# Stick-breaking scores without the mask's matmul, a later multiply by the retention's row factors, and weights kept in the row tiles

## The chip, the cores and the metric

The kernel runs on one core of one Trainium2 chip. The metric is the device time of one execution in microseconds (us). TensorE (PE in the profile) multiplies matrices, VectorE (DVE) and ScalarE (ACT) do the elementwise work, GpSimd (POOL) a few small operations, and SyncE (SP) and ScalarE issue the transfers.

## The reference

Two layers. Each normalises the residual, multiplies it by one wide weight matrix, feeds the columns to four groups of heads (retention, Mamba-2 SSD, stick-breaking attention, a read of memory tokens), multiplies each group by its gate, and projects back. The change touches two of the groups:

```python
def stick_breaking(q, k, v):                 # 4 heads of 128, 512 positions, blocks of 128 queries
        logits = jnp.einsum('bthd,bshd->bhts', q_blk, k).astype(jnp.float32) * scale
        q_pos = i * SB_BLOCK + jnp.arange(SB_BLOCK)
        causal = key_pos[None, :] < q_pos[:, None]
        log_beta = jax.nn.log_sigmoid(logits)
        log_1mb = jnp.where(causal, jax.nn.log_sigmoid(-logits), 0.0)
        tail = lax.cumsum(log_1mb, axis=3, reverse=True) - log_1mb
        w = jnp.where(causal, jnp.exp(log_beta + tail), 0.0)
        return jnp.einsum('bhts,bshd->bthd', w.astype(v.dtype), v)

def retention(q, k, v):                      # 4 heads of 128; after y = intra + inter, per position and head:
    mu = jnp.mean(y, axis=-1, keepdims=True)
    var = jnp.mean(jnp.square(y - mu), axis=-1, keepdims=True)
    y = (y - mu) * lax.rsqrt(var + NORM_EPS)
```

A weight of stick-breaking is exp(logit minus the sum of softplus(logit) over the keys from this one up to the query, the query itself left out), and zero for keys at or behind the query.

## The kernel before

**Products.** Every product of float32 data is three matmuls: each operand is split into a rounded part h and a remainder l (`split`: ScalarE's cast, L286, then VectorE's subtraction, L287), and `mm3` adds h·h, h·l and l·h. Weights arrive as `raw` tiles of 1 MB, are split into `wh` and `wl` (128x1024 each), and a projection is a run of matmuls into a `pj` bank of PSUM; the heads' own products go to `mx` banks. There are four banks of each kind.

**Order.** The code is written in units of one projection. A head's later steps are put off by `defer(n, ...)`, which calls them n units later, so that projections stand between a head's steps. The tile framework then orders each engine's instructions by a list scheduler which plays the program through with its own cost table; the order on an engine is fixed before the program runs. An instruction waits for its data and, where it writes, for its tile's slot: `s` tiles have 33 slots, `y` 16 and `r` (the row tiles) 9.

**Stick-breaking head** (`sb_head`). The head's q is scaled and split (ACT L555, DVE L556), its k is split (L286, L287). For each block t of 128 queries, n = 128(t+1) keys: three matmuls give the logits in an `mx` bank, and a fourth, in bf16, multiplies an identity by a 128x128 block of large negative numbers above the diagonal and adds it on the diagonal block (L641). Then Abs (ACT L643), Exp and Ln (ACT L255), max(b,0)+u (DVE L646, softplus), the running sum from the last key back (DVE L647, a scan), b−u (DVE L649), and Exp (ACT L255). The four blocks' weights lie in three `s` tiles. Three units later they are transposed on PE (L661) and split, and a unit later multiplied by v.

**Retention head** (`ret_head2`, `ret_head3`). The head's y is copied (ACT L740), its squares are summed over the head's 128 channels: two halves added (DVE L744), split into z (ACT L746, DVE L747), and a matmul with a column of ones gives a row (`mx<-r,onesr`). `row_rstd` copies the row (ACT L707), sends it through SP as 32x16 (L709), adds eps and takes the power −1/2 on POOL (L710, L711), writes it to DRAM (L713) and reads it back to all 128 partitions as rB (L715, `r<-row`). Five units after the matmul `scaled` (L757) multiplies y by rB on VectorE. The heads' chains overlap, so L757 of one head stands in VectorE's queue beside L744 and L747 of a later one.

Other names in the rows: L696 to L699 rope; L808, L810, L813 the SSD convolution; L821 and L953 gates; L856, L857, L859 the SSD decay blocks (DVE, POOL, ACT); L730 the retention's causal select on POOL.

Of the kernel before, what the change touches and what calls it, by code (L numbers as in the profile page):

```python
# [8 lines left out]
F32 = mybir.dt.float32  # L9
# [3 lines left out]
ALU = mybir.AluOpType  # L13
# [3 lines left out]
P = 128  # L17
SEQ = 512
NT = SEQ // P
# [4 lines left out]
HEADS = 4  # L24
# [4 lines left out]
NEG = -1e30  # L29
# [94 lines left out]
    return np.ascontiguousarray(t.T.reshape(KC, P, -1).transpose(1, 0, 2).reshape(P, -1))  # L124


CO = dict(ident=0, tri=128, ones=256, neg=384, cos=512, sin=1024, ginv=1536, reps=1552)
NCON = 1552 + 64
RP, RJ = 32, 16


def shape_constants():
    c = np.zeros((P, NCON), np.float32)
    i = np.arange(P)
    c[:, 0:128] = np.eye(P)
    c[:, 128:256] = i[:, None] <= i[None, :]
    c[:, 256:384] = 1.0
    c[:, 384:512] = np.where(i[None, :] >= i[:, None], NEG, 0.0)
    inv = np.float32(10000.0) ** (-np.arange(0, HD, 2, dtype=np.float32) / np.float32(HD))
    ang = (np.arange(SEQ, dtype=np.float32)[:, None] * inv[None, :].astype(np.float32)).T  # L140
    c[:, 512:1024] = np.concatenate([np.cos(ang), np.cos(ang)])
    c[:, 1024:1536] = np.concatenate([np.sin(ang), -np.sin(ang)])
    gam = 1.0 - 2.0 ** (-5.0 - np.arange(HEADS, dtype=np.float64))
    m = np.arange(SEQ, dtype=np.float64)
    gi = gam[None, :] ** (-m[:, None]) * SCALE
    c[:, 1536:1552] = gi.reshape(NT, P, HEADS).transpose(1, 0, 2).reshape(P, 16)
    er = EPS * gam[None, :] ** (-2.0 * m[:, None])
    c[:RP, 1552:1616] = er.reshape(RP, RJ, HEADS).transpose(0, 2, 1).reshape(RP, HEADS * RJ)
    return c


# [4 lines left out]
class Pair:  # L156


    def __init__(self, K, cols=512, tag="s"):
        h, l = K.new(cols, F32R, tag), K.new(cols, F32R, tag)  # L160
        self.h, self.l, self.hf = h[:], l[:], h[:].bitcast(F32)
# [6 lines left out]
class Builder:  # L168
# [4 lines left out]
    def __init__(self, tc, pools, args, taps=None):  # L173
        self.tc, self.nc = tc, tc.nc
        self.a = args
        self.taps = taps or {}
        self.fix, self.slots, self.small, self.wp, self.ps, self.dr = pools
        self.n = self.unit = 0
        self.todo, self.tanhs = [], []
        self.C = self.fixed(NCON + DEPTH * NPAR, F32, "consts")  # L180
        self.b16 = self.fixed(2 * P, BF16, "b16")
        self.onesr = self.fixed(P, F32R, "onesr")
        self.mhalf = self.fixed(RJ, F32, "mhalf")
        self.eps4 = self.fixed(RJ, F32, "eps4")
        self.nc.gpsimd.memset(self.mhalf[:], -0.5)
        self.nc.gpsimd.memset(self.eps4[:], EPS)

# [46 lines left out]
    def con(self, name, n, parts=P):  # L234
        return self.C[:parts, CO[name]:CO[name] + n]

    def par(self, l, name, i, n=1):
        o = NCON + l * NPAR + PO[name] + i
        return self.C[:, o:o + n]
# [37 lines left out]
    def mm(self, out, lhsT, rhs, start, stop):  # L277
        return self.nc.tensor.matmul(out, lhsT, rhs, start=start, stop=stop)  # L278
# [350 lines left out]
    def sb_head(self, h, v):  # L629
        nc = self.nc  # L630
        q = self.scaled_pair(self.proj_b(), SCALE)
        k = self.pair(self.proj_b())
        w = [t[:, c] for t, c in self.packed([P * (t + 1) for t in range(NT)], self.buf)]
        for t in range(NT):
            n = P * (t + 1)
            ts = slice(P * t, P * t + P)
            b = self.mx()[:, :n]
            self.mm(b, q.h[:, ts], k.h[:, :n], True, False)
            self.mm(b, q.h[:, ts], k.l[:, :n], False, False)
            self.mm(b, q.l[:, ts], k.h[:, :n], False, False)  # L640
            self.mm(b[:, P * t:n], self.b16[:, 0:P], self.b16[:, P:2 * P], False, True)  # L641
            u = w[t]
            nc.scalar.activation(u, b, AF.Abs)  # L643
            self.act1(u, u, AF.Exp, scale=-1.0)
            self.act1(u, u, AF.Ln, bias=1.0)
            nc.vector.scalar_tensor_tensor(out=u, in0=b, scalar=0.0, in1=u, op0=ALU.max, op1=ALU.add)  # L646
            nc.vector.tensor_tensor_scan(out=u[:, ::-1], data0=u[:, ::-1], data1=u[:, ::-1], initial=0.0,  # L647
                                         op0=ALU.add, op1=ALU.bypass)
            nc.vector.tensor_sub(u, b, u)  # L649
            self.act1(u, u, AF.Exp)  # L650
        y = self.buf(tag="y")
        self.defer(3, self.sb_head2, h, v, w, y)
        return y
# [96 lines left out]
    def ret_head3(self, h, z, y):  # L750
        nc = self.nc
        vb = self.mx()[0:1]
        self.mm(vb, self.onesr[:, 0:1], z[:], True, True)
        self.defer(5, self.scaled, y, self.row_rstd(vb, self.con("reps", HEADS * RJ, RP)[:, RJ * h:RJ * h + RJ]))

    def scaled(self, y, rB):
        self.nc.vector.tensor_mul(y, y, rB)  # L757


    def dt_chain(self, l, u):  # L760
# [17 lines left out]
    def dt_sums(self, l, da, delta):  # L778
# [17 lines left out]
        hp = self.small.tile([P, 40], F32, tag="hp", name=self.name("hp"), bufs=2)[:]  # L796
        o = NCON + l * NPAR
        nc.vector.tensor_scalar(out=hp, in0=self.C[:, o:o + 40], scalar1=0.5, scalar2=None, op0=ALU.mult)
# [273 lines left out]
    def start(self):  # L1072

        nc = self.nc
        self.warm_up()
        nc.sync.dma_start(self.C[:, NCON:NCON + DEPTH * NPAR], self.a["params"])
        self.w_load(1)
        xs = [self.load_x(0)]
        self.w_load(2)
        preB = self.bcast_row(self.a["pre_norm_g"][0:1])  # L1080
        nc.sync.dma_start(self.C[:, 0:4 * P], self.a["consts"][:, 0:4 * P])
        xs += [self.load_x(1), self.load_x(2)]
        self.mem_tiles()
        self.w_prefetch(1)
        for i in range(4):
            self.mem_pairs(0, i)
        k = [self.pj(), self.pj()]

        def keys(h):
            self.proj_b(self.mx_, N_MEM, k[h // 2][:, N_MEM * (h % 2):N_MEM * (h % 2) + N_MEM])  # L1090
        keys(0)
        self.w_prefetch(2)
        self.w_load(3)
        xs.append(self.load_x(3))
        nc.sync.dma_start(self.C[:, 4 * P:NCON], self.a["consts"][:, 4 * P:NCON])
        keys(1)
        self.w_prefetch(4)
        self.w_load(4)
        keys(2)
        a = [self.normed_a(xs[0])]  # L1100
        self.w_prefetch(5)
        hn = [self.normed_b(a[0], preB)]
        keys(3)
        self.mem_squares()
        self.w_prefetch(6)
        self.mem_add()
        a.append(self.normed_a(xs[1]))
        hn.append(self.normed_b(a[1], preB))

        def v0():  # L1110
            a.append(self.normed_a(xs[2]))
            self.turned(hn[0], 0)
        v = [self.proj_a(self.mx_, 2, between=[v0])[0]]
        self.w_prefetch(7)
        hn.append(self.normed_b(a[2], preB))
        self.turned(hn[1], 1)
        a.append(self.normed_a(xs[3]))
        self.mem_cols()
        self.w_prefetch(8)
        hn.append(self.normed_b(a[3], preB))  # L1120

        def v1():
            self.turned(hn[2], 2)
        v.append(self.proj_a(self.mx_, 2, between=[v1])[0])
        row = self.to_rows(self.mcol, 2)
        self.w_prefetch(10)
        self.turned(hn[3], 3)
        nc.scalar.copy(self.mrow[:], row)
        self.w_load(5)
        for i in range(2):  # L1130
            self.mem_v2(v[i])
        self.w_prefetch(12)
        for i in range(2):
            self.mem_k2(k[i])
        self.w_load(6)
        nc.vector.tensor_copy(self.b16[:, 0:P], self.con("ident", P))
        nc.vector.tensor_copy(self.b16[:, P:2 * P], self.con("neg", P))
        nc.vector.tensor_copy(self.onesr[:], self.con("ones", P))

    def layer(self, l):  # L1140
# [32 lines left out]
def lay_out(x, mem, pre_norm_g, post_norm_g, w_in, conv_w, conv_b, dt_bias, a_log, d_skip, ssd_norm_g, mem_norm_g,  # L1173
            w_mem_kv, w_out):
    return {
        "x": x.reshape(SEQ, D),
        "memT": features_first(mem.reshape(N_MEM, D)),
        "pre_norm_g": pre_norm_g,
        "post_norm_g": post_norm_g,
        "wts": pack_weights(w_in, w_mem_kv, w_out),  # L1180
        "params": pack_params(conv_w, conv_b, dt_bias, a_log, d_skip, ssd_norm_g, mem_norm_g).reshape(P, DEPTH * NPAR),
        "consts": shape_constants(),
    }
# [14 lines left out]
```

## Time and profile before

| | |
|---|---|
| time, 3 runs | 961.94 us median (961.93 to 963.8) |
| profiled execution | 961.89 us, of which the span from the first to the last instruction is 960.2 us and 1.69 us lie outside |
| PE matmul, busy | 949.8 us (99% of the span), 5151 instructions |
| PE weight load | 812.6 us (85%) |
| DVE / ACT / POOL | 657.4 us (68%) / 456.8 us (48%) / 104.4 us (11%, 160 instructions) |
| granted TensorE clock | 0.998, 9 in every slice |

The busy time of PE counts matmuls that overlap, so it hides short gaps: a matmul's record is longer than the distance to the next one's start. Gaps are read from the starts in the timeline. In a row of the timeline the first number is the start, the second the duration, xN a run of N equal instructions, and brackets at the end give the time the engine stood idle before it and what released it.

### The profile page before, as it was taken

How to read it: one execution, taken by the hardware profiler on the slowest of the kernel's cores; microseconds unless marked ns; L12 is line 12 of the kernel's file. 1: busy time of each engine (PE TensorE's matmuls, PEld its weight loads, DVE VectorE, ACT ScalarE, POOL GpSimd, SP SyncE). 2: the span in 40 equal slices, each digit the busy share in tenths (PEclk: the TensorE clock that was granted, in tenths of full speed). 3: DMA queues.
4: the chain of work that ended last, by engine and by line, in shares of the span. 5: the costliest groups of instructions: out<-in, count | busy, mean ns of one | idle time of the engine just before them, and what ended most of it. 6: DMA issues, size and time to landing. Idle time of an engine off the chain costs nothing.

```text
span 960.2 us, 13253 instructions
## 1 busy us (share of the span) xinstructions
PE 949.8 (99%) x5151; PEld 812.6 (85%) x5151; DVE 657.4 (68%) x1056; ACT 456.8 (48%) x844; POOL 104.4 (11%) x160
## 2 busy tenths in 40 slices
PE   9999999999999999999999999999999999999997
PEld 7998889988887888888899888898888878888885
DVE  5855567767777796854487465768777968877443
ACT  6544566534554342643465345665344543435341
POOL 1100000001231201100040000000003421102001
PEclk9999999999999999999999999999999999999999
DMA  9442212122232524344344222112222333423502
GB/s 347 149 147 80 88 45 88 45 88 88 91 108 99 165 88 121 115 160 142 120 170 184 89 88 71 62 45 88 77 78 85 134 105 116 120 91 120 195 25 87
DMA packets 26734, 105.79 MB, mean 110 GB/s; under 512 B 4144, under 2 KB 4400, under 8 KB 17456
## 3 DMA queue, kind: packets, MB, share of 16 engines
q10 hardware_dynamic: 10224, 73.44, 21.8%
q1 hardware_dynamic: 16448, 31.52, 10.0%
q8 instruction: 40, 0.66, 0.3%
q14 instruction: 22, 0.18, 0.1%
HBM read 100.63 MB, written 4.28 MB: 109 GB/s over the span
## 4 chain that ended last, share of the span: by engine, by line
PE 88%; DVE 5%; DMA 3%; ACT 1%; issue 1%; POOL 1%; DVEq 0%; SPq 0%; ACTq 0%; POOLq 0%
PE pj L278 65%; PE mx L278 22%; DVE s L647 1%; DMA r<-row 1%; PE mx L599 1%; PE mx L449 1%; DMA mem<-memT 1%; DMA s<-acs 1%; DVE wl L287 1%; DMA t<-r 1%; POOL t L711 1%; DVE s L810 1%; DVE s L646 0%; PE mx L661 0%; DVE s L287 0%
## 5 line engine op out<-in xcount | busy, mean ns | idle before, releaser
L278 PE MATMUL pj<-hTh,wh 128*128 128x512 f32 x704 | 277.5, 394 | 0.0
L278 PE MATMUL pj<-hTl,wh 128*128 128x512 f32 x704 | 276.6, 393 | 0.0
L278 PE MATMUL pj<-hTh,wl 128*128 128x512 f32 x704 | 275.4, 391 | 0.0
L287 DVE TENSOR_TENSOR wl<-raw,wh 128x1024 fp32r<-128x1024 f32 (+2 forms) x155 | 183.7, 1190 | 114.2 <-ACT wh L286 107.3
L286 ACT CAST wh<-raw 128x1024 fp32r<-128x1024 f32 (+2 forms) x155 | 158.0, 1025 | 178.9 <-PE pj L278 153.7
L278 PEld LDWEIGHTS pj<-hTh,wl 128*128 128x128 f32 x704 | 132.3, 188 | 26.7
L278 PEld LDWEIGHTS pj<-hTh,wh 128*128 128x128 f32 x704 | 132.3, 188 | 26.4
L278 PEld LDWEIGHTS pj<-hTl,wh 128*128 128x128 f32 x704 | 132.4, 188 | 25.7
L278 PE MATMUL pj<-wh,s 128*128 128x512 f32 (+1 forms) x384 | 99.8, 355 | 0.0
L278 PE MATMUL mx<-s,s 128*128 128x256 f32 (+4 forms) x616 | 97.5, 310 | 0.3
L278 PEld LDWEIGHTS mx<-s,s 128*128 128x128 f32 (+1 forms) x616 | 84.6, 178 | 12.9 <-issue 3.1
L278 PE MATMUL mx<-wh,s 128*128 128x512 f32 x256 | 79.2, 389 | 0.0
L278 PEld LDWEIGHTS pj<-wh,s 128*128 128x128 f32 x384 | 66.1, 189 | 10.5
L730 POOL TENSOR_SCALAR_AFFINE_SELECT s<-s 128x128 fp32r<-128x128 f32 x64 | 21.2, 363 | 420.6 <-DVE s L287 420.6
L278 PE MATMUL pj<-wl,s 128*128 128x512 f32 (+1 forms) x192 | 63.4, 354 | 0.0
L278 PE MATMUL pj<-wh,hTh 128*128 128x256 f32 (+1 forms) x208 | 60.3, 290 | 0.5 <-DVE s L556 0.5
L287 DVE TENSOR_TENSOR s<-mx,s 128x512 fp32r<-128x512 f32 (+2 forms) x86 | 42.1, 517 | 26.0 <-ACT s L286 25.6
L278 PE MATMUL pj<-wl,hTh 128*128 128x256 f32 (+1 forms) x208 | 59.5, 286 | 0.0
L278 PE MATMUL pj<-wh,hTl 128*128 128x256 f32 (+1 forms) x208 | 58.5, 284 | 0.0
L278 PEld LDWEIGHTS mx<-wh,s 128*128 128x128 f32 x256 | 48.1, 188 | 10.0
L286 ACT CAST s<-mx 128x512 fp32r<-128x512 f32 (+2 forms) x86 | 36.7, 456 | 40.1 <-PE mx L278 24.1
L287 DVE TENSOR_TENSOR s<-y,s 128x512 fp32r<-128x512 f32 x64 | 41.3, 688 | 19.7 <-ACT s L286 14.0
(167 smaller groups left out, 1324.5 us busy)
## 6 DMA issues: line engine op xcount, KB each, us to landing
raw<-wts ACTq DMA_DIRECT2D x69, 1024.0 KB, 4.8
s<-x SPq DMA_DIRECT2D x24, 256.0 KB, 3.7
s<-acs SPq DMA_DIRECT2D x16, 256.0 KB, 6.1
raw<-wts SPq DMA_DIRECT2D x3, 1024.0 KB, 8.3
r<-row SPq DMA_DIRECT2D x12, 256.0 KB, 3.9
s<-acs SPq DMA_DIRECT2D x16, 128.0 KB, 6.7
x<-s SPq DMA_DIRECT2D x8, 256.0 KB, 2.0
out<-s SPq DMA_DIRECT2D x8, 256.0 KB, 2.0
```

The source lines that it names most:

```text
L278: return self.nc.tensor.matmul(out, lhsT, rhs, start=start, stop=stop)
L286: self.nc.scalar.copy(h, src)
L287: self.nc.vector.tensor_sub(l, src, hf)
L449: x = self.nc.tensor.transpose(b[:, P * j:P * j + P], hn[i][:, P * j:P * j + P], self.con("ident", P))
L599: nc.tensor.transpose(b[:, P * t:P * t + P], w[t // 2][:, o:o + P], self.con("ident", P))
L647: nc.vector.tensor_tensor_scan(out=u[:, ::-1], data0=u[:, ::-1], data1=u[:, ::-1], initial=0.0, op0=ALU.add, op1=ALU.bypass)
L711: nc.gpsimd.tensor_tensor(out=c, in0=c, in1=self.mhalf[:RP], op=ALU.pow)
L730: nc.gpsimd.affine_select(out=d, in_=d, pattern=[[1, P]], compare_op=ALU.is_ge, fill=0.0, base=0, channel_multiplier=-1)
L810: nc.vector.scalar_tensor_tensor(out=acc[:, s:], in0=b[:, :SEQ - s], scalar=tap(3 - s), in1=acc[:, s:], op0=ALU.mult, op1=ALU.add)
```

## The change

1. The mask's matmul (L641) is gone. The scan now multiplies the running sum by a row of ones and zeros (`run`, 512 new columns among the constants, in place of the 128 of `neg`) before it adds the next softplus, so that the sum starts anew at every key from the one just before the query on. After the last Exp, GpSimd's affine_select puts zeros at and above the diagonal of the diagonal block: 32 new POOL instructions of 128x128, and 32 matmuls with their 32 weight loads fewer. Two casts that filled `b16` at the start go too.
2. The weights lie in `r` tiles (9 slots) rather than `s` tiles (33), three a head.
3. `scaled` is put off by 7 units instead of 5, and is kept in program order.

The scheduler's order follows from these. Three places show it, all on VectorE in the first layer (the second repeats them). Names with numbers are tiles; the lines after the change are those of the new file, two or three higher from L661 on.

First place: the start of stick-breaking head 0. `wl270` is the l part of a weight tile, `s243` and `s249` are head 1's q and k, L646, L647, L649 head 0's chain. Before:

```order
L287 TENSOR_TENSOR wl270_1556<-raw214_1249,wh269_1555 128x1024
L646 SCALAR_TENSOR_TENSOR s229_1314<-mx232_1317,s229_1314 128x128
L647 SCALAR_TENSOR_TENSOR s229_1314<-s229_1314 128x128
L649 TENSOR_TENSOR s229_1314<-mx232_1317,s229_1314 128x128
L556 SCALAR_TENSOR_TENSOR s243_1406<-pj238_1374,s242_1405 128x512
L646 SCALAR_TENSOR_TENSOR s229_1314<-mx233_1329,s229_1314 128x256
L647 SCALAR_TENSOR_TENSOR s229_1314<-s229_1314 128x256
L646 SCALAR_TENSOR_TENSOR s230_1315<-mx234_1341,s230_1315 128x384
L649 TENSOR_TENSOR s229_1314<-mx233_1329,s229_1314 128x256
L287 TENSOR_TENSOR s249_1447<-pj245_1417,s248_1446 128x512
```

After:

```order
L556 SCALAR_TENSOR_TENSOR s243_1404<-pj238_1372,s242_1403 128x512
L287 TENSOR_TENSOR s249_1445<-pj245_1415,s248_1444 128x512
L287 TENSOR_TENSOR wl270_1554<-raw214_1247,wh269_1553 128x1024
L646 SCALAR_TENSOR_TENSOR r229_1312<-mx232_1315,r229_1312 128x128
L647 SCALAR_TENSOR_TENSOR r229_1312<-consts_72,r229_1312 128x128
L649 TENSOR_TENSOR r229_1312<-mx232_1315,r229_1312 128x128
L646 SCALAR_TENSOR_TENSOR r229_1312<-mx233_1327,r229_1312 128x256
L647 SCALAR_TENSOR_TENSOR r229_1312<-consts_72,r229_1312 128x256
L646 SCALAR_TENSOR_TENSOR r230_1313<-mx234_1339,r230_1313 128x384
```

Head 1's q and k (L556 and the L287 of s249) move ahead of head 0's whole chain, out of its middle.

Second place: the third retention head's sum of squares. `r507`, `r508` and `r509` are that head's, `y395` and `y426` the y of the first and the second head, `r439` and `r479` their rB, `wl540` a weight's l part. Before:

```order
L744 TENSOR_TENSOR r507_2836<-r507_2836,r508_2837 64x512
L757 TENSOR_TENSOR y426_2446<-y426_2446,r479_2700 128x512
L813 SCALAR_TENSOR_TENSOR s528_2949<-s528_2949,s527_2948 128x512
L810 SCALAR_TENSOR_TENSOR s532_2985<-pj529_2956,hp134_776,s532_2985 128x511
L810 SCALAR_TENSOR_TENSOR s532_2985<-pj529_2956,hp134_776,s532_2985 128x510
L747 TENSOR_TENSOR r509_2841<-r507_2836,r509_2841 64x512
L810 SCALAR_TENSOR_TENSOR s532_2985<-pj529_2956,hp134_776,s532_2985 128x509
L287 TENSOR_TENSOR wl540_3042<-raw490_2770,wh539_3041 128x1024
```

After (L746, L749, L760, L813 and L816 are what L744, L747, L757, L810 and L813 were):

```order
L816 SCALAR_TENSOR_TENSOR s528_2946<-s528_2946,s527_2945 128x512
L760 TENSOR_TENSOR y395_2290<-y395_2290,r439_2510 128x512
L813 SCALAR_TENSOR_TENSOR s532_2983<-pj529_2954,hp134_774,s532_2983 128x511
L746 TENSOR_TENSOR r507_2833<-r507_2833,r508_2834 64x512
L813 SCALAR_TENSOR_TENSOR s532_2983<-pj529_2954,hp134_774,s532_2983 128x510
L813 SCALAR_TENSOR_TENSOR s532_2983<-pj529_2954,hp134_774,s532_2983 128x509
L287 TENSOR_TENSOR wl540_3039<-raw490_2768,wh539_3038 128x1024
L749 TENSOR_TENSOR r509_2838<-r507_2833,r509_2838 64x512
L816 SCALAR_TENSOR_TENSOR s533_2984<-s533_2984,s532_2983 128x512
```

The multiply that stands here is now that of the first head (y395) and not of the second; `wl540` and one more instruction of the convolution, which stood behind L747, now stand ahead of L749.

Third place: the fourth retention head's sum of squares (`r535` to `r537`), before, where `y465` with `r522` is the third head's:

```order
L287 TENSOR_TENSOR wl561_3147<-raw526_2946,wh560_3146 128x1024
L757 TENSOR_TENSOR y465_2632<-y465_2632,r522_2915 128x512
L744 TENSOR_TENSOR r535_3008<-r535_3008,r536_3009 64x512
L813 SCALAR_TENSOR_TENSOR s558_3114<-s558_3114,s557_3113 128x512
L810 SCALAR_TENSOR_TENSOR s563_3152<-pj559_3121,hp134_776,s563_3152 128x511
L747 TENSOR_TENSOR r537_3013<-r535_3008,r537_3013 64x512
L810 SCALAR_TENSOR_TENSOR s563_3152<-pj559_3121,hp134_776,s563_3152 128x510
L810 SCALAR_TENSOR_TENSOR s563_3152<-pj559_3121,hp134_776,s563_3152 128x509
```

After:

```order
L287 TENSOR_TENSOR wl561_3145<-raw526_2943,wh560_3144 128x1024
L746 TENSOR_TENSOR r535_3005<-r535_3005,r536_3006 64x512
L816 SCALAR_TENSOR_TENSOR s558_3111<-s558_3111,s557_3110 128x512
L760 TENSOR_TENSOR y426_2444<-y426_2444,r479_2698 128x512
L813 SCALAR_TENSOR_TENSOR s563_3150<-pj559_3119,hp134_774,s563_3150 128x511
L749 TENSOR_TENSOR r537_3010<-r535_3005,r537_3010 64x512
L813 SCALAR_TENSOR_TENSOR s563_3150<-pj559_3119,hp134_774,s563_3150 128x510
```

L746 is no longer behind a multiply; the one that stands ahead of L749 is the second head's (y426 with r479), and the third head's comes nine rows behind L749.

On PE the matmul of the row (`mx<-r,onesr`) comes 8 projection matmuls earlier for the second head, 5 later for the third and 2 later for the fourth. On SP one of the loads of the SSD decay rows (`s<-acs`) moves ahead of the fourth head's `r<-row`.

The diff, cut to its core:

```diff
-CO = dict(ident=0, tri=128, ones=256, neg=384, cos=512, sin=1024, ginv=1536, reps=1552)
-NCON = 1552 + 64
+CO = dict(ident=0, tri=128, ones=256, run=384, cos=896, sin=1408, ginv=1920, reps=1936)
+NCON = 1936 + 64
...
-    c[:, 384:512] = np.where(i[None, :] >= i[:, None], NEG, 0.0)
+    c[:, 384:896] = np.arange(512)[None, :] < 383 + i[:, None]
...
-        w = [t[:, c] for t, c in self.packed([P * (t + 1) for t in range(NT)], self.buf)]
+        w = [t[:, c] for t, c in self.packed([P * (t + 1) for t in range(NT)], lambda: self.buf(tag="r"))]
+        run = self.con("run", SEQ)
...
-            self.mm(b, q.l[:, ts], k.h[:, :n], False, False)
-            self.mm(b[:, P * t:n], self.b16[:, 0:P], self.b16[:, P:2 * P], False, True)
+            self.mm(b, q.l[:, ts], k.h[:, :n], False, True)
...
-            nc.vector.tensor_tensor_scan(out=u[:, ::-1], data0=u[:, ::-1], data1=u[:, ::-1], initial=0.0,
-                                         op0=ALU.add, op1=ALU.bypass)
+            nc.vector.tensor_tensor_scan(out=u[:, ::-1], data0=run[:, SEQ - n:][:, ::-1], data1=u[:, ::-1], initial=0.0,
+                                         op0=ALU.mult, op1=ALU.add)
             nc.vector.tensor_sub(u, b, u)
             self.act1(u, u, AF.Exp)
+            d = u[:, P * t:]
+            nc.gpsimd.affine_select(out=d, in_=d, pattern=[[-1, P]], compare_op=ALU.is_gt, fill=0.0, base=0, channel_multiplier=1)
...
-        self.defer(5, self.scaled, y, self.row_rstd(vb, self.con("reps", HEADS * RJ, RP)[:, RJ * h:RJ * h + RJ]))
+        self.defer(7, self.scaled, y, self.row_rstd(vb, self.con("reps", HEADS * RJ, RP)[:, RJ * h:RJ * h + RJ]))
 
     def scaled(self, y, rB):
-        self.nc.vector.tensor_mul(y, y, rB)
+
+        self.tc.keep_in_program_order(self.nc.vector.tensor_mul(y, y, rB))
...
-        nc.vector.tensor_copy(self.b16[:, 0:P], self.con("ident", P))
-        nc.vector.tensor_copy(self.b16[:, P:2 * P], self.con("neg", P))
```

## Rows read from the trace of the kernel before

**Rows 1.** The page: busy time of each engine, share of the span, instructions.

```profile
PE 949.8 (99%) x5151; PEld 812.6 (85%) x5151; DVE 657.4 (68%) x1056; ACT 456.8 (48%) x844; POOL 104.4 (11%) x160
```

**Rows 2.** Waits of PE: line waited for, total us, times, longest us.

```profile
PE mx L278 <- DVE r L747: 1.8, 2, 0.9
```

**Rows 3.** Timeline of PE around a mask of stick-breaking head 0.

```profile
136.82 0.39 PE L278 MATMUL pj<-hTh,wh 128*128 128x512 f32 x1
137.05 0.44 PE L278 MATMUL mx<-s,s 128*128 128x128 f32 x3
137.34 0.23 PE L278 MATMUL mx<-b 128*128 128x128 bf16 x1
137.38 0.47 PE L278 MATMUL pj<-hTl,wh 128*128 128x512 f32 x1
137.69 0.51 PE L278 MATMUL mx<-s,s 128*128 128x256 f32 x3
```

**Rows 4.** Timeline of PE at two stops of the stick-breaking stage.

```profile
149.81 0.51 PE L278 MATMUL mx<-s,s 128*128 128x256 f32 x3
150.57 0.38 PE L278 MATMUL pj<-wh,hTh 128*128 128x256 f32 x1 [0.24 <-DVE s L556]
150.79 0.28 PE L278 MATMUL pj<-wl,hTh 128*128 128x256 f32 x1
150.91 0.28 PE L278 MATMUL pj<-wh,hTl 128*128 128x256 f32 x1
...
165.84 0.27 PE L661 MATMUL mx<-consts,s 128*128 128x128 f32 x1
166.23 0.73 PE L278 MATMUL mx<-s,s 128*128 128x512 f32 x2
```

**Rows 5.** Timeline of DVE ahead of the first of these stops.

```profile
149.82 0.69 DVE L556 SCALAR_TENSOR_TENSOR s<-pj,s 128x512 fp32r<-128x512 f32 x1 [0.85 <-ACT s L555]
```

**Rows 6.** Timeline of PE at the fourth retention head's row.

```profile
307.41 0.39 PE L278 MATMUL pj<-hTl,wh 128*128 128x512 f32 x1
308.69 0.39 PE L278 MATMUL mx<-r,onesr 128*1 128x512 f32 x1 [0.89 <-DVE r L747]
```

**Rows 7.** Timeline of DVE ahead of the third and the fourth head's row.

```profile
285.19 1.12 DVE L757 TENSOR_TENSOR y<-y,r 128x512 f32<-128x512 f32 x1
...
288.39 0.69 DVE L747 TENSOR_TENSOR r<-r,r 64x512 fp32r<-64x512 f32 x1
...
305.37 0.69 DVE L757 TENSOR_TENSOR y<-y,r 128x512 f32<-128x512 f32 x1 [5.42 <-DMA r<-row]
...
307.95 0.69 DVE L747 TENSOR_TENSOR r<-r,r 64x512 fp32r<-64x512 f32 x1
```

**Rows 8.** Timeline of ACT: the fourth head's squares, which L744 adds.

```profile
298.60 1.19 ACT L743 ACTIVATE r<-mx 64x512 f32<-64x512 f32 x2
```

**Rows 9.** Timeline of PE at the third head's row.

```profile
290.53 0.40 PE L278 MATMUL mx<-r,onesr 128*1 128x512 f32 x1
```

**Rows 10.** Line L730: duration ns min/median/max, first and last start.

```profile
L730 POOL TENSOR_SCALAR_AFFINE_SELECT s<-s x64: 284/294/1262, 216.9 to 750.6; 128x128 fp32r<-128x128 f32 x64
```

**Rows 11.** Groups by line and form: busy us, mean ns | idle before.

```profile
L287 DVE TENSOR_TENSOR wl<-raw,wh 128x1024 fp32r<-128x1024 f32 x145 | 177.1, 1224 | 110.9 <-ACT wh L286 104.2 <-PE mx L278 6.2
L647 DVE TENSOR_TENSOR_SCAN s<-s 128x512 f32<-128x512 f32 x8 | 9.8, 1219 | 0.0
```

**Rows 12.** Timeline of POOL and DVE where selects meet a weight's split.

```profile
257.72 2.32 POOL L730 TENSOR_SCALAR_AFFINE_SELECT s<-s 128x128 fp32r<-128x128 f32 x3
257.78 1.31 DVE L287 TENSOR_TENSOR wl<-raw,wh 128x1024 fp32r<-128x1024 f32 x1
```

**Rows 13.** Windows: us, busy PE, PEld, DVE, ACT, POOL (instructions), clock, DMA, GB/s.

```profile
160.00:180.00 20.00, 19.89 (x160) 19.00 (x160) 16.24 (x29) 14.14 (x31) 0.00 (x0) 1.00 0.17 56
```

**Rows 14.** Timeline of ACT: last Exp of stick-breaking head 3.

```profile
185.36 0.63 ACT L255 ACTIVATE s<-s 128x512 f32<-128x512 f32 x1
```

**Rows 15.** Timeline of PE: last transposes of head 3.

```profile
189.79 0.73 PE L661 MATMUL mx<-consts,s 128*128 128x128 f32 x5
```

More of the change, by code (lines that the diff above doesn't have):

```diff
@@ L137, in shape_constants @@
     c[:, 256:384] = 1.0
-    c[:, 384:512] = np.where(i[None, :] >= i[:, None], NEG, 0.0)
+    c[:, 384:896] = np.arange(512)[None, :] < 383 + i[:, None]
     inv = np.float32(10000.0) ** (-np.arange(0, HD, 2, dtype=np.float32) / np.float32(HD))
     ang = (np.arange(SEQ, dtype=np.float32)[:, None] * inv[None, :].astype(np.float32)).T
-    c[:, 512:1024] = np.concatenate([np.cos(ang), np.cos(ang)])
-    c[:, 1024:1536] = np.concatenate([np.sin(ang), -np.sin(ang)])
+    c[:, 896:1408] = np.concatenate([np.cos(ang), np.cos(ang)])
+    c[:, 1408:1920] = np.concatenate([np.sin(ang), -np.sin(ang)])
     gam = 1.0 - 2.0 ** (-5.0 - np.arange(HEADS, dtype=np.float64))
@@ L145, in shape_constants @@
     gi = gam[None, :] ** (-m[:, None]) * SCALE
-    c[:, 1536:1552] = gi.reshape(NT, P, HEADS).transpose(1, 0, 2).reshape(P, 16)
+    c[:, 1920:1936] = gi.reshape(NT, P, HEADS).transpose(1, 0, 2).reshape(P, 16)
     er = EPS * gam[None, :] ** (-2.0 * m[:, None])
-    c[:RP, 1552:1616] = er.reshape(RP, RJ, HEADS).transpose(0, 2, 1).reshape(RP, HEADS * RJ)
+    c[:RP, 1936:2000] = er.reshape(RP, RJ, HEADS).transpose(0, 2, 1).reshape(RP, HEADS * RJ)
     return c
@@ L180, in __init__ @@
         self.C = self.fixed(NCON + DEPTH * NPAR, F32, "consts")
+        self.mhalf = self.fixed(RJ, F32, "mhalf")
+        self.eps4 = self.fixed(RJ, F32, "eps4")
         self.b16 = self.fixed(2 * P, BF16, "b16")
         self.onesr = self.fixed(P, F32R, "onesr")
-        self.mhalf = self.fixed(RJ, F32, "mhalf")
-        self.eps4 = self.fixed(RJ, F32, "eps4")
         self.nc.gpsimd.memset(self.mhalf[:], -0.5)
@@ L1080, in start @@
         preB = self.bcast_row(self.a["pre_norm_g"][0:1])
-        nc.sync.dma_start(self.C[:, 0:4 * P], self.a["consts"][:, 0:4 * P])
+        nc.sync.dma_start(self.C[:, 0:3 * P], self.a["consts"][:, 0:3 * P])
         xs += [self.load_x(1), self.load_x(2)]
@@ L1094, in start @@
         xs.append(self.load_x(3))
-        nc.sync.dma_start(self.C[:, 4 * P:NCON], self.a["consts"][:, 4 * P:NCON])
+        nc.sync.dma_start(self.C[:, 3 * P:NCON], self.a["consts"][:, 3 * P:NCON])
         keys(1)
```

## The prediction

> **What bounds the kernel now.** I read the page first: PE is busy for 949.8 us [rows 1] of a span of 960.2, and the granted clock is full throughout. So the time is PE's own work plus the places where PE stops, and a change counts by what it takes out of PE's queue or by the stops it makes and ends; the idle time of VectorE or GpSimd by itself is worth nothing. Next I read the waits of PE, which name VectorE's L747 as the largest releaser [rows 2], and then the timeline of PE, since the record of a matmul is longer than its distance to the next: a projection matmul of 512 columns is 0.39 long and the next starts 0.23 later (136.82 to 137.05, [rows 3]), and at 256 columns 0.12 later (150.79 to 150.91, [rows 4]). A larger distance is a stop.
>
> There are three kinds inside the layers. At 150.57 PE needs a scaled q of the next stick-breaking head: three matmuls of 256 columns from 149.81 on should have ended their turns at 150.17, so 0.40 is lost [rows 4]; VectorE did L556 at 149.82 after standing idle for ScalarE's L555 [rows 5]. At 166.23 the product with v follows one transpose, started at 165.84, whose turn is about 0.12: 0.27 lost [rows 4]. At 308.69 the fourth retention head's row should have started at 307.41 + 0.23 = 307.64: 1.05 lost [rows 6]. The second layer has the same three; per layer that is 0.40 + 0.27 + 1.05 = 1.72, together 3.44 us. How the 1.05 comes about is in VectorE's timeline: it stands idle 5.42 us for a transfer of the third head's rB, then does L757 at 305.37, and L744, two instructions of the convolution and L747 come behind it [rows 7].
>
> **The masks.** 32 matmuls with their loads go. In rows 3 the mask starts at 137.34 and the projection matmul behind it at 137.38, 0.04 later; but that matmul is followed after 0.31 instead of 0.23. So a mask costs 0.04 + 0.08 = 0.12, and 32 of them 3.84 us, all on PE's path. Bounds: the 0.04 alone would make 1.3, the mask's own record of 0.23 [rows 3] 7.4. I take 0.12, which is measured where the mask stands between ordinary neighbours. The Trainium skill (TensorE: Matmul & The Clock Gate, section Wait — 56ns, not 53.3ns?) gives N/2.4 GHz plus about 2.5 ns from start to start, so by estimate 56 ns for 128 columns; by it the masks would be worth 1.8 us and the sum below 957.1. The distances in rows 3 say twice that, and they decide.
>
> **The multiply by rB.** Third place of the order: L744 (now L746) no longer follows a multiply, and the one ahead of L747 (now L749) uses the second head's rB. That factor had landed by 285.19, where the multiply ran without a wait [rows 7]. So nothing there waits for a transfer any more. The squares that L744 adds are done at 298.60 + 1.19 = 299.79 [rows 8], and VectorE is idle from 299.95 on (305.37 less 5.42, [rows 7]). From there L749 stands behind four instructions of some 0.69 each: about 299.95 + 2.8 = 302.7 instead of 307.95, against a demand that comes at 307.64 or later. Both 1.05 stops go, with about 4 us to spare. What is late next is the third head. Second place: L749 there has `wl540` (1.22, [rows 11]) and one convolution step (about 0.69) more ahead of it, so it ends near 288.39 + 0.69 + 1.9 = 291.0 [rows 7], while PE wants it five projection matmuls later than before, at 290.53 + 5 x 0.23 = 291.7 [rows 9]. It fits by 0.7; if VectorE is late by more, up to about 0.5 a layer returns here. The multiplies themselves cost VectorE what they did, 0.69 to 1.12 [rows 7]; y is wanted only by the gates and the output projection long after, so their delay is free. On SP one load of the decay rows goes ahead of the fourth `r<-row`; its multiply now stands some twenty rows later, so that is free too.
>
> **The stick-breaking chain.** Per block VectorE has the same three instructions. The scan has the same two inputs in SBUF and the same length, and I take its 1.22 for 512 keys as unchanged [rows 11]; the trace does not show the multiply-and-add form, so the price may be anything between a little less and twice that (rival below). The order (first place) takes head 1's q and k out of the middle of head 0's chain, and on ScalarE head 2's q (L555) is ahead of head 1's last Exp. Since L556 stood idle 0.85 for L555 [rows 5], its earlier place ends the 0.40 stop; played forward with the new order it is ready about 0.6 before PE. For the 0.27 stop the same play comes out between 0.3 late and even. I leave 0.5 us over both layers for this and the third head's row.
>
> **The selects.** 32 instructions of GpSimd between the last Exp and the transposes: 0.28 to 1.26 each, 0.29 in the middle [rows 10]. The tightest place is head 3, where the last Exp ends at 185.36 + 0.63 = 185.99 [rows 14] and the last transposes start at 189.79 [rows 15]: 3.8 us hide even the longest. GpSimd has nothing else to do in this stage [rows 13]. If that cover were gone each select would cost PE its length, 4.6 us in a layer. The selects can also hold up VectorE: where three of them met a split of a weight, the split took 1.31 and they 2.32 together [rows 12], against 1.22 and 3 x 0.29 [rows 10, 11]. The Trainium skill (SBUF — State Buffer, section Who interferes with whom) has the rule: a VectorE instruction with two inputs in SBUF and a GpSimd one that reads SBUF lock each other out for the whole of the one that came first. The trace agrees. I price it at nothing for the forecast, since VectorE has 3.8 of 20 us free even in the busiest stretch (16.24 busy, [rows 13]), and make it a rival.
>
> **The rest** is costed at nothing: three row tiles a head in nine slots mean that head 3 needs head 0's tiles back, whose transposes stand on PE well before head 3's scores; the larger table of constants is loaded while the first projections run and first read by the scans of this stage; two casts less at the start lie on VectorE beside PE's work.
>
> **Sum.** 961.89 (the profiled execution, 1.69 above its span and 0.05 below the median of the runs) - 3.84 - 3.44 + 0.5 = 955.1 us.
>
> **Rivals.**
> First, *the locks come back as stops of PE*. If each of a head's four selects puts 0.29 into VectorE's chain, a head is 1.16 late; less the 0.6 of spare time that makes 0.56 for eight heads, 4.5 us: 959.6; with half the heads touched, 957.4. For it: the chain already stops PE twice a layer, and the selects of one block run beside the scan of the next. Against it: most of the work beside them reads PSUM, and only an overlap at the wrong moment costs. I take 958.5.
> Second, *the masks were nearly hidden*, as PE fills its gap with the next load: then only the stops count, 961.89 - 3.44 + 0.5 = 958.9. Against it stand the distances of rows 3.
> Third, *a row still waits*: the third head's row takes over the fourth's stop, 1.05 a layer; 957.2. For it: only 0.7 of spare time there.
> Fourth, on the other side, *the scan in its new form is longer*. A head's four scans sum to about 3.3 (1.22 for 512 keys, estimated by length for the shorter ones). They lie in the chain between scores and transposes. The gain of 6.8 over eight heads is 0.85 a head; with 0.6 spare the change turns to a loss once a head's scans grow by 1.45, that is by some 45%. At twice the length, 2.7 for eight heads is 21.6: about 976.7. For it: two arithmetic steps where one was a bypass. Against it: inputs and length stay as they were; nothing else in the trace bears on it.
>
> **Chances.** Forecast 0.61 (its own range 954.0 to 956.5); the locks 0.17; masks hidden 0.07; a row waits 0.09; the longer scan 0.06. The low end of the range is a mask at 0.14 and no stop left: 961.89 - 4.4 - 3.44 = 954.0; the high end takes in the locks' own price, 959.7. A measurement of this kernel can tell about 0.2%, 1.9 us, from no change. Faster by more than that: the forecast, masks hidden, a row, and two thirds of the locks, 0.87; within it, the rest of the locks and a scan a third longer, 0.08; slower 0.05.
>
> **What would show it.** Right: no `mx<-b` of 128 columns on PE, projection matmuls 0.23 apart behind the scores; no wait of PE for L749; no idle time of VectorE before L760; new selects mostly near 0.29 and finished before the transposes. Wrong: a scan of 512 keys far from 1.22; waits of PE for L556, for the splits behind the transposes or for POOL; a stop before the third head's row; the transposes waiting for a select.

## The result, and the profile after

The changed kernel takes 954.76 us (median of 6 runs, 954.34 to 956.56) against 961.93 (6 runs): a ratio of 0.9928 with a 95% interval of 0.9915 to 0.9941. The forecast was 955.1. Its profiled execution took 954.53, with a span of 952.8 against 960.2. The page of the changed kernel, busy time by engine:

```profile
span 952.8 us, 13237 instructions
PE 944.1 (99%) x5119; PEld 812.3 (85%) x5119; DVE 655.9 (69%) x1054; ACT 456.4 (48%) x844; POOL 117.1 (12%) x192
```

Against [rows 1] 32 matmuls are gone from PE and 32 instructions more stand on GpSimd. The waits of PE, as in [rows 2]:

```profile
PE mx L278 <- POOL b L190: 1.2, 1, 1.2
PE mx L278 <- DVE s L287: 0.9, 2, 0.4
PE pj L278 <- ACT s L492: 0.2, 1, 0.2
```

The wait for L747 (L749 now) and that for L556 are gone; a new one for a split, L287, is there twice. The timeline of PE shows the places of [rows 3, 4 and 6]: behind a head's scores, at the first stop, at the second, at the third head's row and at the fourth's.

```profile
135.95 0.39 PE L278 MATMUL pj<-hTh,wl 128*128 128x512 f32 x1
136.18 0.52 PE L278 MATMUL mx<-s,s 128*128 128x256 f32 x3
136.53 0.40 PE L278 MATMUL pj<-hTh,wh 128*128 128x512 f32 x1
136.76 0.40 PE L278 MATMUL pj<-hTl,wh 128*128 128x512 f32 x1
...
148.73 0.28 PE L278 MATMUL pj<-wh,hTh 128*128 128x256 f32 x1
...
163.44 0.27 PE L663 MATMUL mx<-consts,r 128*128 128x128 f32 x1
164.15 0.73 PE L278 MATMUL mx<-s,s 128*128 128x512 f32 x2 [0.43 <-DVE s L287]
...
289.17 0.40 PE L278 MATMUL mx<-r,onesr 128*1 128x512 f32 x1
...
305.60 0.40 PE L278 MATMUL mx<-r,onesr 128*1 128x512 f32 x1
```

The projection matmul behind the scores is followed after 0.23 (136.53 to 136.76) as predicted, where it was 0.31. The first stop (150.57 before) has no wait any more. The second has grown: 163.44 + 0.12 to 164.15 is 0.59 where it was 0.27, in both layers. Neither row waits. VectorE's timeline ahead of these places, as in [rows 7]:

```profile
162.43 1.21 DVE L647 TENSOR_TENSOR_SCAN r<-consts,r 128x512 f32<-128x512 f32 x1
163.56 0.86 DVE L287 TENSOR_TENSOR s<-mx,s 128x384 fp32r<-128x384 f32 x2
...
286.24 0.69 DVE L749 TENSOR_TENSOR r<-r,r 64x512 fp32r<-64x512 f32 x1
...
297.63 0.68 DVE L746 TENSOR_TENSOR r<-r,r 64x512 f32<-64x512 f32 x1
...
298.84 0.68 DVE L760 TENSOR_TENSOR y<-y,r 128x512 f32<-128x512 f32 x1
...
300.21 0.69 DVE L749 TENSOR_TENSOR r<-r,r 64x512 fp32r<-64x512 f32 x1
```

The multiply at 298.84 waits for nothing, and L749 is done at 300.90, 4.7 us ahead of PE's 305.60; the third head's is done at 286.93, 2.2 ahead of 289.17. The scan of 512 keys takes 1.21, as before [rows 11]. The stop at 164.15 waits for the splits that stand behind that scan. The new selects, by the line's view, and the last one of head 3, on GpSimd:

```profile
L652 POOL TENSOR_SCALAR_AFFINE_SELECT r<-r x32: 289/295/1952, 128.2 to 651.1; 128x128 f32<-128x128 f32 x32
```

```profile
183.54 1.95 POOL L652 TENSOR_SCALAR_AFFINE_SELECT r<-r 128x128 f32<-128x128 f32 x1 [5.71 <-ACT r L255]
```

One took 1.95, longer than the 1.26 that [rows 10] had shown, just where the cover was counted: it ends at 185.49, and PE runs on until the transposes at 187 without a wait.

**Where the time went, by stage.** The projections are the same 3504 matmuls in all these kernels, so the time from the n-th to the m-th of them can be compared, worked out from their starts in the two traces. The time before the 60th is left out: it differed by up to 2.3 us between the profiled executions, and goes by the execution more than by the kernel (last section). Gains against the kernel before, in us:

| | layer 1, stick-breaking and before (60 to 1060) | layer 1, retention (1060 to 1300) | layer 2 | sum |
|---|---|---|---|---|
| changed kernel | 1.99 | 1.29 | 3.55 | 6.83 |

The four masks of head 0 can be read by themselves: they stand in one run of scores (124.34 to 125.78 before), and up to the 500th projection matmul the two kernels differ by 0.01. At the first projection matmul behind the scores the gain is 0.37, at the second it is 0.45, since the first is followed after 0.24 where it was 0.32; layer 2 has the same 0.37 and 0.45. That is 0.11 a mask. (The mask in [rows 3] is that of the next head, not of head 0 as is said there.) PE there, before and after:

```profile
125.81 0.47 PE L278 MATMUL pj<-hTh,wh 128*128 128x512 f32 x1
126.13 0.39 PE L278 MATMUL pj<-hTl,wh 128*128 128x512 f32 x1
...
124.92 0.39 PE L278 MATMUL pj<-hTh,wh 128*128 128x512 f32 x1
125.16 0.40 PE L278 MATMUL pj<-hTl,wh 128*128 128x512 f32 x1
```

### The profile page after: what moved, and what is told of

The parts are those of the page before. It is cut to its first block, busy times and chain, and to the rows that moved or that the text cites. A ratio compares the mean times of both kernels' runs of the same rounds, so it can differ in the third digit from the quotient of the medians.

```text
span 952.8 us, 13237 instructions
## 1 busy us (share of the span) xinstructions
PE 944.1 (99%) x5119; PEld 812.3 (85%) x5119; DVE 655.9 (69%) x1054; ACT 456.4 (48%) x844; POOL 117.1 (12%) x192
## 4 chain that ended last, share of the span: by engine, by line
PE 96%; DVE 2%; DMA 1%; ACT 1%; DVEq 0%; SPq 0%; issue 0%; POOLq 0%; POOL 0%; ACTq 0%
PE pj L278 71%; PE mx L278 22%; PE mx L599 1%; PE mx L449 1%; DMA mem<-memT 1%; PE mx L663 1%; DVE r L647 1%; DVE r L646 0%; PE mx L874 0%; DVE wl L287 0%; DVE r L649 0%; DVE s L287 0%; ACT r L643 0%; PE mx L894 0%; DVEq L1195 0%; DVE t L683 0%
## 5 line engine op out<-in xcount | busy, mean ns | idle before, releaser
L287 DVE TENSOR_TENSOR wl<-raw,wh 128x1024 fp32r<-128x1024 f32 (+2 forms) x155 | 183.6, 1190 | 124.0 <-ACT wh L286 123.4
L278 PE MATMUL mx<-s,s 128*128 128x256 f32 (+4 forms) x616 | 95.0, 309 | 0.9 <-DVE s L287 0.9
L287 DVE TENSOR_TENSOR s<-mx,s 128x512 fp32r<-128x512 f32 (+2 forms) x86 | 41.9, 515 | 24.2 <-ACT s L286 23.7
L287 DVE TENSOR_TENSOR s<-y,s 128x512 fp32r<-128x512 f32 x64 | 41.2, 686 | 19.7 <-ACT s L286 14.0
L286 ACT CAST s<-y 128x512 fp32r<-128x512 f32 x64 | 36.6, 617 | 29.6 <-PE mx L278 22.0
```

What stands on the lines that cost most here:

```text
L286: self.nc.scalar.copy(h, src)
L287: self.nc.vector.tensor_sub(l, src, hf)
```

## The experiments

The three parts can be put together in all ways, since the scheduler's order of the stick-breaking stage depends only on the first and third part, and of the retention's rows mostly on the second (row_tiles_only is the exception). The sums by stage, in us gained against the kernel before (masks out, row tiles, multiply in program order):

| run | masks out | row tiles | in order | layer 1 stick-br. | layer 1 ret. | layer 2 | sum | median us |
|---|---|---|---|---|---|---|---|---|
| before | no | no | no | 0 | 0 | 0 | 0 | 962.1 |
| masks_only | yes | no | no | 0.60 | -2.79 | 0.43 | -1.76 | 964.87 |
| later_mul_only | no | no | yes | -0.01 | 1.29 | 1.55 | 2.83 | 959.0 |
| row_tiles_only | no | yes | no | 0.92 | 1.32 | 2.43 | 4.67 | 957.25 |
| s_tiles | yes | no | yes | 0.59 | 1.29 | 2.15 | 4.03 | 958.94 |
| defer7_free | yes | yes | no | 1.96 | -1.31 | 2.08 | 2.73 | 960.08 |
| mask_back | put back | yes | yes | 0.94 | 1.32 | 2.52 | 4.78 | 958.29 |
| changed kernel | yes | yes | yes | 1.99 | 1.29 | 3.55 | 6.83 | 954.76 |

**The masks' part alone** (masks_only): the change without these two edits.

```diff
-        w = ... lambda: self.buf(tag="r"))]
+        w = ... self.buf)]
-        self.defer(7, self.scaled, y, ...)
+        self.defer(5, self.scaled, y, ...)
-        self.tc.keep_in_program_order(self.nc.vector.tensor_mul(y, y, rB))
+        self.nc.vector.tensor_mul(y, y, rB)
```

> Part 1 of the change alone: no mask matmul, scan with the row of ones and zeros, 32 selects; weights stay in the s tiles and the multiply by rB as before (its place in VectorE's order is that of the kernel before, ahead of L744 of the fourth head). Theory (each mask costs PE 0.12 us, the row stop is the multiply's alone): 961.9 - 3.9 = 958.0, between 957.4 and 958.6, with the two stops of about 1.05 before the fourth head's row still there. Rival A (masks nearly hidden): 961 or more. Rival B (selects and VectorE lock each other out): 959.5 or more.

Measured: 964.87 us, slower than before (ratio 1.0022, interval 1.001 to 1.0035). The waits of PE, and the timeline of PE and of VectorE at the fourth head's row:

```profile
PE mx L278 <- DVE r L749: 3.3, 2, 2.3
PE mx L278 <- ACT s L286: 2.1, 4, 0.8
```

```profile
311.07 0.40 PE L278 MATMUL mx<-r,onesr 128*1 128x512 f32 x1 [2.33 <-DVE r L749]
311.30 0.40 PE L278 MATMUL pj<-hTh,wl 128*128 128x512 f32 x1
311.54 0.42 PE L278 MATMUL pj<-hTh,wh 128*128 128x512 f32 x1
311.76 0.63 PE L278 MATMUL pj<-hTl,wh 128*128 128x512 f32 x1
312.18 0.63 PE L278 MATMUL pj<-hTh,wl 128*128 128x512 f32 x1
...
314.74 0.59 PE L278 MATMUL pj<-hTh,wl 128*128 128x512 f32 x1
315.17 0.40 PE L278 MATMUL pj<-hTh,wh 128*128 128x512 f32 x1
```

```profile
307.75 0.69 DVE L760 TENSOR_TENSOR y<-y,r 128x512 f32<-128x512 f32 x1 [6.86 <-DMA r<-row]
```

The theory's 957.4 to 958.6 was missed; two things were not in it. In the stick-breaking stage new stops behind the transposes (0.38, 0.48 and 1.02 in each layer, four of the six waits on ScalarE's splits) take back most of the masks' gain: 0.60 is left of some 2.0. And the row stop is worse than before in layer 1: the transfer of rB took 6.13 by the chain of waits (4.41 before; its landing released the multiply in [rows 7]), the stop grew from 1.05 to 2.5, and behind it PE ran at half its clock: eight matmuls start 0.43 apart instead of 0.23, a loss of another 1.6. In layer 2 the stop is 1.12, about what it was. The windows of this run show the granted clock there:

```profile
300.00:310.00 10.00, 8.73 (x39) 6.91 (x37) 3.14 (x5) 2.94 (x6) 0.17 (x1) 1.00 0.39 133
310.00:320.00 10.00, 8.93 (x38) 7.38 (x39) 9.62 (x14) 4.12 (x7) 3.34 (x2) 0.83 0.21 70
```

The columns are those of [rows 13]; the clock is the third from the end. A direct test of the masks as PE's work is head 0, above: they do cost PE, so the rival that they were hidden falls too.

**The later multiply alone** (later_mul_only).

```diff
-        self.defer(5, self.scaled, y, ...)
+        self.defer(7, self.scaled, y, ...)
-        self.nc.vector.tensor_mul(y, y, rB)
+        self.tc.keep_in_program_order(self.nc.vector.tensor_mul(y, y, rB))
```

> Part 2 alone: the multiply by rB put off by 7 units and kept in program order; masks and s tiles as before. VectorE's order shows the second head's multiply, not the third's, ahead of the fourth head's L747. Theory (PE waits because L744 and L747 stand behind a multiply that waits for a transfer): both stops go, 961.9 less 2.1 to 2.6, 959.3 to 959.8, no idle time of VectorE before the multiply. Rival (the stops end only through the other order that the missing masks bring): 961.4 to 962.3.

Measured: 959.0 us (ratio 0.9968, 0.9957 to 0.9979), a little better than the 959.3 to 959.8 of the theory, 2.83 by stage, no wait for L747. Apart from the first 12 us, PE's only waits are the two that the kernel before has for L556:

```profile
PE pj L278 <- DVE s L556: 0.5, 2, 0.2
```

The theory holds: the multiply's place makes the row stops.

**Which half of that edit does it** (defer7_free, defer5_kept).

```diff
 # defer7_free, against the changed kernel
-        self.tc.keep_in_program_order(self.nc.vector.tensor_mul(y, y, rB))
+        self.nc.vector.tensor_mul(y, y, rB)
 # defer5_kept, against the changed kernel
-        self.defer(7, self.scaled, y, ...)
+        self.defer(5, self.scaled, y, ...)
```

> The changed kernel without the instruction to keep the multiply in program order (still 7 units late). VectorE's order at the retention's rows is then that of the kernel before. Theory (keeping program order is what moves the multiply, the 7 units are nothing by themselves): the row stops return, 1.05 a layer or more as the transfer lands later against a faster PE: 957.0 to 961.5, most likely 958.5; if the stop of the first layer passes 2 us, the granted clock falls behind it as it did with the masks' part alone. Rival (the 7 units do it): 954.3 to 955.6.

> The changed kernel with the multiply put off by 5 units as before, but kept in program order. VectorE's order has L746 and L749 of each head ahead of the multiply of the head before. Theory (program order is what counts): 954.3 to 955.6, as the changed kernel, no row stop. Rival (7 units are needed): the multiply waits for its transfer ahead of something PE needs, 956.5 or more.

Measured: 960.08 and 955.06 us. By stage 2.73 and 6.78, against 6.83. Without program order the row stops are back, 2.37 and 1.24 over the nominal distance; with it, 5 units are as good as 7. So the keeping in order is the edit and the number is not. One part of the expectation for defer7_free failed: its first stop passed 2 us, and the granted clock did not fall behind it (last section). The timeline of VectorE in defer5_kept shows L749 ahead of the multiply, which again waits for nothing:

```profile
299.25 0.68 DVE L749 TENSOR_TENSOR r<-r,r 64x512 fp32r<-64x512 f32 x1
...
303.92 0.69 DVE L760 TENSOR_TENSOR y<-y,r 128x512 f32<-128x512 f32 x1
```

**The tiles** (row_tiles_only, s_tiles).

```diff
 # row_tiles_only, against the kernel before
-        w = ... self.buf)]
+        w = ... lambda: self.buf(tag="r"))]
 # s_tiles, against the changed kernel: the reverse
```

> Part 3 alone: the kernel before with the weights in row tiles, masks and multiply as before. Theory (tiles matter only through the order of the stick-breaking stage): row stops stay; the stage gains or loses at most the 1.3 us of its stops: 960.7 to 963. Rival (nine slots are too few and PE waits for row tiles): 964 or more.

> The changed kernel with the stick-breaking weights back in s tiles. Its order in the stick-breaking stage is that of the run with the masks' part alone, its order in the retention stage that of the changed kernel. Theory (the row tiles decide the order of the stage, and with it the stops of PE that eat the masks' gain): the stage loses what it lost there, 1.4 us a layer, so 954.8 + 2.8 = 957.6, between 956.9 and 958.4, with stops before the products with v. Rival (the tiles are neutral; the masks' part alone was slow only through the row stop): 954.3 to 955.6.

Measured: 957.25 us (ratio 0.9953, 0.994 to 0.9966) and 958.94. The first is the largest surprise: the tiles alone, costed at nothing, gain 4.67. All waits of PE in its profile lie in the first 12 us:

```profile
PE mx L278 <- POOL b L190: 1.2, 1, 1.2
PE pj L278 <- ACT s L492: 1.2, 2, 0.8
```

Not only the two stops of the stick-breaking stage are gone, the row's is as well. The multiply still waits there, but L744 is now ahead of it, the transfer lands earlier, and PE asks later; VectorE and PE at that place:

```profile
297.52 0.67 DVE L744 TENSOR_TENSOR r<-r,r 64x512 f32<-64x512 f32 x1
301.70 0.69 DVE L757 TENSOR_TENSOR y<-y,r 128x512 f32<-128x512 f32 x1 [3.51 <-DMA r<-row]
...
304.16 0.68 DVE L747 TENSOR_TENSOR r<-r,r 64x512 fp32r<-64x512 f32 x1
```

```profile
287.33 0.40 PE L278 MATMUL mx<-r,onesr 128*1 128x512 f32 x1
...
306.00 0.40 PE L278 MATMUL mx<-r,onesr 128*1 128x512 f32 x1
```

L747 is done at 304.85, 1.15 ahead of PE. From the third row to the fourth are 18.7 us, against 290.53 to 307.64 [rows 6, 9], 17.1, where PE would have asked before. That is the tiles' doing through the order the scheduler finds with them; why the pool changes its choice as far as the retention was not taken apart and stays open. Putting the s tiles back into the changed kernel costs 2.80 by stage, the 2.8 expected (the whole time is higher by a slower start): its stops in the stick-breaking stage are those of masks_only.

**The mask put back** (mask_back): a matmul of zeros in its place, with the new scan and the selects kept; its stick-breaking order is that of row_tiles_only.

```diff
-            self.mm(b, q.l[:, ts], k.h[:, :n], False, True)
+            self.mm(b, q.l[:, ts], k.h[:, :n], False, False)
+            self.mm(b[:, P * t:n], self.b16[:, 0:P], self.b16[:, P:2 * P], False, True)
```

> The changed kernel with a bf16 matmul of 128x128 put back behind each block's scores; it adds zeros, so the result is unchanged. Its order in the stick-breaking stage is that of the run with the row tiles alone (no stop there), with the multiply in program order. Theory (0.12 us a matmul on PE's path, stops follow the order alone): 32 x 0.12 = 3.8 more, less the 1.2 of the stops: 957.4, between 956.8 and 958.2. Rival (the matmul is nearly hidden): 953.6 to 954.8.

Measured: 958.29 us, just above what was expected; by stage 4.78 against 6.83, 2.05 more, where 2.0 to 3.4 was expected. No stop is left in its layers, while the changed kernel has two of 0.59: so 32 matmuls cost 2.05 + 1.18 = 3.23, 0.10 each, if the two orders are worth the same to PE apart from their stops. They need not be: row_tiles_only gains 0.92 in the first column, where the stops that it ended come to 0.67. Head 0 gave 0.11; the changed kernel against the one before, 1.99 in the first column less the 0.08 by which its stops are shorter, gives 0.12 for each of 16. So the forecast's 0.12 is at the upper end of what the runs show, and up to a fifth too high. One thing that it left out is in the changed kernel's timeline: behind scores of 128 columns, as in [rows 3], the first projection matmul takes 0.28 (135.21 to 135.49) without any mask, and not 0.23, so that mask cost 0.04 + 0.03 = 0.07; behind 256 columns it takes 0.23 (136.53 to 136.76), and there the 0.12 holds.

**The selects** (no_selects, double_selects). Order on PE and VectorE as in the changed kernel; no_selects leaves out the zeros of the causal mask.

```diff
 # no_selects: these two lines removed; double_selects: the second line twice
             d = u[:, P * t:]
             nc.gpsimd.affine_select(out=d, in_=d, ...)
```

> The changed kernel without its 32 new selects (the weights at and above the diagonal stay, so that part of the causal mask is left out); the order on every other engine is the same. Theory (selects are hidden; the new stop of 0.59 us a layer comes from the splits behind the scan of 512 keys): within 0.5 us of the changed kernel, 954.3 to 955.2, the stop stays. Rival (the selects lock VectorE out and make the stop): 1 us or more faster, 953.6 or less, the stop gone or much shorter.

> The changed kernel with every new select done twice, the same order on PE and VectorE. Theory (hidden): 954.3 to 955.3, the same. Rival (VectorE locked out for the length of a select): 32 x 0.29 = 9.3 us of locked time more, of which, if half lands on PE's path, 959; some splits and scans longer than 1.3 us.

Measured: 955.58 and 955.72 us, 0.4 above what was expected; by stage 6.81 and 6.73 against 6.83 (both profiled executions had the slow start of the last section). The stop is 0.59 without them and 0.64 with twice as many. So 32 selects cost nothing that shows, and 32 more about 0.1. The theory holds; the locks are not what made the stop.

**Two tries to end the last stop** (head3_later, head2_later).

```diff
 # head3_later
-        self.defer(1, self.sb_head3, h, v, wT, y)
+        self.defer(2, self.sb_head3, h, v, wT, y)
 # head2_later
-        self.defer(3, self.sb_head2, h, v, w, y)
+        self.defer(4, self.sb_head2, h, v, w, y)
```

> The changed kernel with the product with v (sb_head3) put off by 2 units instead of 1, so that some 28 or more matmuls of 256 columns stand between a head's last transpose and its product. Theory (the stop of 0.59 a layer is the split of the transposed weights standing in VectorE's queue behind the scan of 512 keys): the stop goes, 954.8 - 1.2 = 953.6, between 953.0 and 954.6. Rival (VectorE is late by more than that in the stage, so that the stop moves to the next head's product): 954.5 to 956.

> The changed kernel with the transposes (sb_head2) put off by 4 units instead of 3; row tiles are held longer, four heads of three tiles against nine slots. Theory: the stop of 0.59 a layer goes or moves; 953.6 to 955. Rival (the row tiles run out: the last head's Abs waits for slots): stops of PE behind scores of the fourth head, 956 or more.

Measured: 963.22 and 958.76 us, both worse (by stage -0.03 and 4.23 in sum). In head3_later the product has its distance, but the scheduler has moved the scan of 512 keys against the transposes, and PE waits at them; VectorE and PE there:

```profile
163.50 1.31 DVE L647 TENSOR_TENSOR_SCAN r<-consts,r 128x512 f32<-128x512 f32 x1
164.73 0.66 DVE L287 TENSOR_TENSOR s<-mx,s 128x512 fp32r<-128x512 f32 x1
165.31 0.15 DVE L684 TENSOR_SCALAR t<-t 128x4 f32<-128x4 f32 x1
```

```profile
163.86 0.38 PE L663 MATMUL mx<-consts,r 128*128 128x128 f32 x2
165.54 0.30 PE L663 MATMUL mx<-consts,r 128*128 128x128 f32 x1 [1.30 <-DVE t L684]
```

The profile names L684, which has no tile of PE's; the split at 164.73, behind the scan, is the likelier releaser, which was not tested. Smaller stops follow it in each layer. In head2_later four new stops of 0.29 to 0.62 a layer stand at the last head. No run beat the changed kernel: masks out in an order without any stop would be worth another 1.18, and none of these orders was it.

## Why the prediction was right

The time came out as forecast, 954.76 against 955.1, by terms that were partly off and made up for one another: the rows gave 0.7 more than their term, the stick-breaking stops 0.7 less. That these two cancel is luck.

- *The masks, 3.84.* Right in kind: they were on PE's path. The size lies between 3.2 (mask_back) and 3.8 (what is left of 6.83 without 2.83 for the rows and 0.16 for the stops); head 0 gives 3.6. A matmul of 128 columns in bf16 between those of float32 cost 0.10 to 0.12 on average here. The page TensorE: Matmul & The Clock Gate of the Trainium skill (Wait — 56ns, not 53.3ns?) would give 0.056, and the measurement decides.
- *The row stops, 2.10.* Right in cause, and too small: the retention stage of layer 1 gained 1.29, the 1.05 and 0.24 of smaller distances behind it, and both layers 2.83 (later_mul_only). L749 was forecast 4 us ahead of PE and was 4.7; the third head's 0.7, and it had 2.2. later_mul_only and defer7_free show the cause from both sides. The edit's 7 units were never needed.
- *The stick-breaking stops, 1.34 less the 0.5 left.* The step that failed is the second stop, played forward as "between 0.3 late and even": it grew to 0.59. The first ended as forecast. Of the 0.84 only 0.16 came. VectorE ran without a gap from 157 to 165 there, so it had nothing to give when PE came earlier.
- *The row tiles, costed at nothing.* This was wrong, and the sum hid it. The cost of the slots was looked at, and their hold on the scheduler's order was not. Alone they are worth 4.67, and on top of the other two 2.80; without them taking the masks out is worth 1.20 with the multiply in order (s_tiles against later_mul_only), with them 2.05. Without that order it is a loss either way, 1.76 and 1.94. The order of the changed kernel, which the forecast read, already held their effect, so the time came out; the attribution of it to parts did not.
- *The selects at nothing.* Right, to 0.1 us. The longest one, 1.95 from 183.54 on, ran beside two subtractions of VectorE with both inputs in SBUF (183.52 to 185.33), which took their ordinary 1.21 and 0.68; so GpSimd was the side that waited, and nobody waited for it. That agrees with the rule in the Trainium skill (SBUF — State Buffer, Who interferes with whom) that the prediction named.
- *The scan unchanged.* Right: 1.21.
- *The start.* The forecast took none; the profiled execution gained 0.47 before its first projection, by chance.

Of the rivals, the locks, the hidden masks and the longer scan are out. A row that still waits is what masks_only and defer7_free became: with stops of 2.5 and 2.37 in layer 1, and in masks_only a fallen clock behind it, dearer than the 1.05 it was priced at.

## What to carry to other kernels

Where a scheduler sets the order, an edit's worth is read from the whole new order, and its parts can't be priced one by one: here one part alone was a loss, and two others each removed the same stop. Taking work off the bounding engine makes it ask earlier for what the others deliver, so first find the waits that a transfer ends, and move whatever stands behind them in the same queue. Compare stages between the same instructions of both traces; whole times hide what a varying start adds.

## What the runs showed of the hardware that was not expected

A wait of 2.33 us on PE was followed by eight matmuls at the lower of its two clocks, 1.2 instead of 2.4 GHz (masks_only, above). So a stop can cost more than its length. It need not: in defer7_free a wait of 2.21 at the same place left the granted clock at 1.00, as the stops of 1.05 in the kernel before did. What makes the difference between 2.21 and 2.33 is not shown. PE and the windows of defer7_free there, columns as in [rows 13]:

```profile
309.53 0.39 PE L278 MATMUL mx<-r,onesr 128*1 128x512 f32 x1 [2.21 <-DVE r L749]
...
310.00:320.00 10.00, 9.97 (x50) 8.20 (x49) 9.44 (x14) 5.04 (x8) 3.75 (x2) 1.00 0.31 106
```

The clock also falls at the start in some executions, and the longer starts go with it: in nine of the thirteen traces the window from 10 to 20 us shows less than 1.00. In mask_back, one of them, the first projections wait longer for the memory tokens' transfer, and then the clock falls. Windows of the kernel before and of mask_back, columns as in [rows 13]:

```profile
0.00:10.00 10.00, 8.55 (x42) 5.71 (x42) 3.19 (x9) 4.59 (x9) 0.59 (x7) 1.00 0.81 273
10.00:20.00 10.00, 9.95 (x76) 9.36 (x77) 7.16 (x12) 9.35 (x18) 1.59 (x3) 1.00 1.03 395
```

```profile
0.00:10.00 10.00, 7.66 (x42) 5.31 (x42) 3.52 (x9) 4.94 (x9) 0.59 (x7) 1.00 0.81 256
10.00:20.00 10.00, 9.95 (x66) 9.43 (x66) 6.79 (x10) 8.96 (x18) 1.59 (x3) 0.83 1.04 407
```

PE is idle 0.9 us longer in the first ten, and gets through ten matmuls fewer in the next ten at a granted clock of 0.83. That is about 2 us, which fits the distance between the lower and the upper of the changed kernel's own times, 954.3 to 954.9 and 956.2 to 956.6. A transfer of 256 KB to all partitions (`r<-row`) took 4.41 in the kernel before, 6.13 in masks_only and 6.06 in defer7_free, at the same place of the program; why it took longer there was not taken apart.
